# A streaming softmax: two loads merged into one, and three transfers released by a part of a group

## The chip, the cores and the metric

The kernel runs on one core of a Trainium2 chip. The metric is the device time of one execution in microseconds (us), the median of several runs. Beside it stands one profiled execution, whose trace gives the span of the program and what each engine and each DMA transfer did in it.

The engines named here are DVE (VectorE), ACT (ScalarE), POOL (GpSimd) and SP (SyncE, which here only waits and issues DMA). PE (TensorE) does nothing in this kernel.

## The reference

A softmax over the last axis of a float32 tensor of 16 x 1024 x 512:

```python
x_max = np.max(x, axis=-1, keepdims=True)
exp_x = np.exp(x - x_max)
return (exp_x / np.sum(exp_x, axis=-1, keepdims=True)).astype(np.float32)
```

Input and output have 33.55 MB each, so 67.11 MB pass between DRAM and the core's memory.

## The kernel before, in words

The 16384 rows of 512 numbers are spread over 128 partitions, so that each partition has 128 rows. In the kernel "row r" means the r-th row of every partition (128 x 512 numbers, 256 KB). Rows are worked on in 16 groups of 8 (`GROUP`): group g is rows 8g to 8g+7. The buffer `held` has room for 12 groups (`RING`, 96 rows), so rows 96 to 127 use the places of rows 0 to 31 again.

Rows are loaded and stored in larger transfers, all on one queue, SP's. `ORDER` lists them: "L" for a load, "S" for a store, with their rows. In this text a transfer is called by its first row: load 0, 16, 32, 48 (16 rows, 4 MB each), load 64 (32 rows, 8 MB), load 96 and 112 (4 MB); store 0, 16, 32, 48 (4 MB), store 64 and 96 (8 MB). The first five (`AHEAD`) are issued at the start, and the rest in the order of the list by SP, each after waiting for what it needs. `BLOCKS` says how rows lie in DRAM: the rows of a block are divided among the partitions so that each partition has one contiguous run, and a transfer of half a block takes half of each run (loads 96 and 112 do, from block 96 to 127).

What each issue waits for, on SP:

- a store waits for the groups in it to be scaled (semaphores `scaled[g]`),
- a load into places that are used again waits for the stores of what was there (`stored`),
- `AFTER` adds a wait: store 0 also waits for group 4, load 96 for group 8, load 112 for group 9, store 48 for group 11. These groups are not in the transfer; the wait only holds the issue back.

SP works through its list in order, so that a wait holds back everything behind it.

Each group goes through four steps, and the names below are used throughout:

- M (L167, DVE): `reduce_max` over the 8 rows, negated, after the load has landed.
- the exponential (L211, ACT): 8 activations, one for each row, in a loop over groups; each also sums its row. ACT takes one group after another and waits for M of the next.
- P's reciprocal (L175, DVE): one over the sums, after ACT's last row of the group.
- P's product (L181, POOL): the 8 rows times the reciprocals, one `tensor_mul` of 128 x 4096. Groups 14 and 15 do it on DVE instead (V14, V15).

The list `VECTOR` gives DVE's order of M, P and V steps. DVE carries it out strictly in this order, so that an M whose load hasn't landed holds back the reciprocals behind it.

Of the kernel before, what the change touches and what calls it, by code (L numbers as in the profile page):

```python
# [13 lines left out]
GROUP = 8  # L14
# [3 lines left out]

BLOCKS = [(0, 16), (16, 32), (32, 48), (48, 64), (64, 96), (96, 128)]
ORDER = [
    ("L", (0, 16)),
    ("L", (16, 32)),
    ("L", (32, 48)),
    ("L", (48, 64)),
    ("L", (64, 96)),
    ("S", (0, 16)),
    ("S", (16, 32)),
# [4 lines left out]
    ("S", (64, 96)),  # L34
    ("S", (96, 128)),
]
AHEAD = 5

AFTER = {("S", 0): 4, ("L", 96): 8, ("L", 112): 9, ("S", 48): 11}

VECTOR = """
    M0 M1 P0 M2 P1 M3 P2 M4 P3 M5 P4 M6 P5 M7 P6 M8 P7 M9 P8 M10 P9 M11
    P10 P11 M12 M13 P12 M14 P13 M15 V14 V15
"""

# [23 lines left out]
@with_exitstack  # L73
def kernel(
    ctx: ExitStack,
    tc: tile.TileContext,
    x: bass.AP,
    out: bass.AP,
):
    nc = tc.nc  # L80
    nc.at_finalize(loads_at_the_head)
    P = nc.NUM_PARTITIONS

    d = x.shape[-1]
    x_rows, out_rows = x.flatten_outer_dims(), out.flatten_outer_dims()
    assert x_rows.shape[0] == GROUPS * GROUP * P

    def in_dram(rows, a, b):

        first, last = next(k for k in BLOCKS if k[0] <= a and b <= k[1])  # L90
        block = rows[first * P : last * P].rearrange("(p r) d -> p r d", p=P)
        return block[:, a - first : b - first, :]

    held = nc.alloc_sbuf_tensor("held", [P, RING, d], F32).ap()
    shift = nc.alloc_sbuf_tensor("shift", [P, GROUPS * GROUP], F32).ap()
    sums = nc.alloc_sbuf_tensor("sums", [P, GROUPS * GROUP], F32).ap()
    recip = nc.alloc_sbuf_tensor("recip", [P, GROUPS * GROUP], F32).ap()

    loads = [k for what, k in ORDER if what == "L"]
    stores = [k for what, k in ORDER if what == "S"]  # L100
    loaded = {k: nc.alloc_semaphore(f"loaded{k[0]}") for k in loads}
    scaled = [nc.alloc_semaphore(f"scaled{g}") for g in range(GROUPS)]
    stored = {k: nc.alloc_semaphore(f"stored{k[0]}") for k in stores}
    maxed = nc.alloc_semaphore("maxed")
    expd = nc.alloc_semaphore("expd")
    to_pool = nc.alloc_semaphore("to_pool")
    to_vector = nc.alloc_semaphore("to_vector")

    def take(engine, semaphore, n):

        engine.wait_ge(semaphore, n).then_inc(semaphore, -n)  # L111

    def rows(a, b):
        assert a // RING == (b - 1) // RING
        return held[:, a % RING : (b - 1) % RING + 1, :]

    def meets(k, a, b):
        return k[0] < b and a < k[1]

    def group(g):  # L120
        return g * GROUP, (g + 1) * GROUP

    def stats(t, g):
        return t[:, g * GROUP : (g + 1) * GROUP]

    def load(k):
        copy = nc.sync.dma_start(out=rows(*k), in_=in_dram(x_rows, *k))
        copy.then_inc(loaded[k], 16)
        return copy

    with tc.manual_schedule():
        for _, k in ORDER[:AHEAD]:
            tc.no_tile_sem_insts.add(load(k).ins.name)
    tc.close()
    tc.compile()  # L138

    taken, done = set(), set()  # L140
    for what, k in ORDER[AHEAD:]:
        for g in range(GROUPS):
            due = AFTER.get((what, k[0])) == g or (what == "S" and meets(k, *group(g)))
            if due and g not in done:
                take(nc.sync, scaled[g], 1)
                done.add(g)
        if what == "L":
            for s in stores:
                if meets(s, k[0] - RING, k[1] - RING) and s not in taken:
                    take(nc.sync, stored[s], 16)  # L150
                    taken.add(s)
            load(k)
        else:
            nc.sync.dma_start(out=in_dram(out_rows, *k), in_=rows(*k)).then_inc(
                stored[k], 16
            )

    seen, given = set(), {}  # L160

    def rowmax(g):
        for k in loads:
            if meets(k, *group(g)) and k not in seen:
                take(nc.vector, loaded[k], 16)
                seen.add(k)
        nc.vector.reduce_max(  # L167
            out=stats(shift, g), in_=rows(*group(g)), axis=AX, negate=True
        ).then_inc(maxed, 1)

    def scale(g, engine, ready):

        if g == 0:
            take(nc.vector, expd, 1)
        ratio = nc.vector.reciprocal(out=stats(recip, g), in_=stats(sums, g))  # L175
        if g:
            ratio.wait_op(expd, g, "sem-ge")
        ratio.then_inc(ready, 1)
        if g == 0:
            take(engine, ready, 1)  # L180
        product = engine.tensor_mul(  # L181
            out=rows(*group(g)),
            in0=rows(*group(g)),
            in1=stats(recip, g).unsqueeze(2).to_broadcast([P, GROUP, d]),
        )
        if g:
            given[ready] = given.get(ready, 0) + 1
            product.wait_op(ready, given[ready], "sem-ge")
        product.then_inc(scaled[g], 1)

    for step in VECTOR.split():
        what, g = step[0], int(step[1:])
        if what == "M":
            rowmax(g)
        elif what == "V":
            scale(g, nc.vector, to_vector)
        else:
            scale(g, nc.gpsimd, to_pool)
    take(nc.vector, expd, GROUPS - 1)
    take(nc.vector, to_vector, given[to_vector])  # L200
    take(nc.gpsimd, to_pool, given[to_pool])


    nc.scalar.preload_act_table(EXP)  # L204

    with nc.scalar.Fori(0, GROUPS) as i:  # L206
        take(nc.scalar, maxed, 1)
        for r in range(GROUP):
            row = held[:, bass.ds(i % (RING // GROUP) * GROUP + r, 1), :]
            at = bass.ds(i * GROUP + r, 1)  # L210
            act = nc.scalar.activation(  # L211
                out=row,
                in_=row,
                func=EXP,
                bias=shift[:, at],
                scale=1.0,
                accum_out=sums[:, at],
            )
        act.then_inc(expd, 1)


    for k in stores:
        if k not in taken:
            take(nc.sync, stored[k], 16)
# [30 lines left out]
```

## Time and profile before

| | us |
|---|---|
| median of 3 runs (lowest to highest) | 159.46 (159.26 to 159.68) |
| profiled execution, its own time | 159.32 |
| its span in the trace | 158.0 |
| DVE, ACT, POOL busy | 83.8, 91.9, 97.9 |
| one product of a group on POOL (L181), mean of 14 | 7.016 |
| one reduction of a group on DVE (L167), mean of 16 | 4.396 |
| one exponential row on ACT (L211), mean of 128 | 0.713 |
| DMA queue q1, share of 16 engines' span | 99.0% |

The span runs from the first instruction to the last; the profiled execution's own time is 1.32 us more. The busy time of an engine counts its compute instructions alone; waiting and issuing DMA is not counted. The DMA share is how much of the time the packets of the 16 DMA engines took. Times in rows of a timeline are counted from the start of the span. A transfer is complete when it has landed, which its semaphore shows.

### The profile page before, as it was taken

To read this page: it belongs to the slowest core of one execution; us is meant where nothing else is said; L and a number is where in the kernel's file an instruction comes from. 1 tells how busy PE (TensorE), PEld (TensorE's weight loads), DVE (VectorE), ACT (ScalarE), POOL (GpSimd) and SP (SyncE) were. 2 spreads that over 40 slices of the span, in tenths; PEclk is the share of its full clock that TensorE was granted. 3 is DMA by queue.
4 is the path that set the end of the run, shared out by engine and by line. 5 is a ranking of instruction groups with operands and counts; after the bars stand their busy time and mean duration, and the time that the engine had idled before them with its cause. 6 is when DMAs were issued, how large, how long until landed. Compare 5 with 4: busy or idle time off the path is not lost. (4 is left out here: it accounts for less than half of the span.)

```text
span 158.0 us, 714 instructions
## 1 busy us (share of the span) xinstructions
DVE 83.8 (53%) x34; ACT 91.9 (58%) x257; POOL 97.9 (62%) x18
## 2 busy tenths in 40 slices
DVE  0008959778977916969760000695976998000000
ACT  1100699999999997499999300049999920000000
POOL 0000009999999999999999999991999600000000
DMA  7999999999969969999999999999999969969976
GB/s 265 465 465 398 398 473 456 398 398 489 572 265 531 498 299 398 456 465 407 398 465 465 373 423 398 431 481 415 398 514 415 531 265 531 498 299 531 465 332 265
DMA packets 1872, 67.11 MB, mean 425 GB/s; under 512 B 208, under 2 KB 208, under 8 KB 208
## 3 DMA queue, kind: packets, MB, share of 16 engines
q1 hardware_dynamic: 1872, 67.11, 99.0%
HBM read 33.55 MB, written 33.55 MB: 425 GB/s over the span
## 5 line engine op out<-in xcount | busy, mean ns | idle before, releaser
L181 POOL TENSOR_TENSOR held<-held,recip 128x4096 f32<-128x4096 f32 x14 | 97.7, 7016 | 26.8 <-POOLq L111 23.0
L211 ACT ACTIVATE held<-held,shift x128 | 90.3, 713 | 32.2 <-ACTq L111 32.2
L167 DVE TENSOR_REDUCE shift<-held 128x8 f32<-128x4096 f32 x16 | 70.2, 4396 | 27.8 <-DVEq L111 27.8
L211 ACT ACTIVATION_READ_ACCUMULATOR held<-held,shift x128 | 24.7, 193 | 0.0
L175 DVE RECIPROCAL recip<-sums 128x8 f32<-128x8 f32 x16 | 3.2, 202 | 22.1 <-ACT held L211 20.2
L181 DVE TENSOR_TENSOR held<-held,recip 128x4096 f32<-128x4096 f32 x2 | 11.4, 5725 | 0.1
L204 ACT ACT_TABLE_LOAD x1 | 1.3, 1283 | 3.5 <-PEq L138 3.5
L239 POOL MEMSET const-float32-0.0<- 128x1 f32 x1 | 0.1, 98 | 0.2 <-issue 0.2
L239 POOL MEMSET const-bfloat16-1.0<- 128x1 bf16 x1 | 0.1, 101 | 0.0
L239 POOL MEMSET const-uint8-127<- 128x1 uint8 x1 | 0.1, 101 | 0.0
L239 POOL MEMSET const-float32-1.0<- 128x1 f32 x1 | 0.1, 98 | 0.0
## 6 DMA issues: line engine op xcount, KB each, us to landing
held<-in_x_dram SPq DMA_DIRECT2D x6, 4096.0 KB, 18.7
out_dram<-held SPq DMA_DIRECT2D x4, 4096.0 KB, 16.5
out_dram<-held SPq DMA_DIRECT2D x2, 27.5
held<-in_x_dram SPq DMA_DIRECT2D x1, 58.4
```

The costliest lines, as they stand in the source:

```text
L167: nc.vector.reduce_max(out=stats(shift, g), in_=rows(*group(g)), axis=AX, negate=True).then_inc(maxed, 1)
L175: ratio = nc.vector.reciprocal(out=stats(recip, g), in_=stats(sums, g))
L181: product = engine.tensor_mul(out=rows(*group(g)), in0=rows(*group(g)), in1=stats(recip, g).unsqueeze(2).to_broadcast([P, GROUP, d]),)
L204: nc.scalar.preload_act_table(EXP)
L211: act = nc.scalar.activation(out=row, in_=row, func=EXP, bias=shift[:, at], scale=1.0, accum_out=sums[:, at],)
L239: nc = _bacc.Bacc("TRN2", target_bir_lowering=False, num_devices=1)
```

## The change

1. Rows 32 to 63 become one block and one load of 8 MB ("load 32" from here on; load 48 is gone). Four transfers are issued ahead, not five. Stores 32 and 48 are still two, and each now takes half of every partition's run in DRAM.
2. In DVE's order, P3 comes ahead of M4.
3. Three products on POOL (groups 4, 8 and 11) are split into two instructions: the first 7, 7 and 6 rows, and the rest. The first of each pair raises a new semaphore `begun`; store 0, load 96 and store 48 wait for it, in place of the whole group. Load 112 still waits for all of group 9. Store 32 still waits for all of groups 4 and 5, and store 64 for all of groups 8 to 11, because these are in them.

On POOL, 14 products become 17 instructions: 11 of 128x4096, two of 128x3584 with 128x512 behind each, and one of 128x3072 with 128x1024 behind it. On SP there is one load less, and the order of the others is the same.

```diff
-BLOCKS = [(0, 16), (16, 32), (32, 48), (48, 64), (64, 96), (96, 128)]
+BLOCKS = [(0, 16), (16, 32), (32, 64), (64, 96), (96, 128)]
 ORDER = [
     ("L", (0, 16)),
     ("L", (16, 32)),
-    ("L", (32, 48)),
-    ("L", (48, 64)),
+    ("L", (32, 64)),
     ("L", (64, 96)),
...
-AHEAD = 5
+AHEAD = 4
...
-AFTER = {("S", 0): 4, ("L", 96): 8, ("L", 112): 9, ("S", 48): 11}
+AFTER = {("L", 112): 9}
+AFTER_FIRST = {("S", 0): 4, ("L", 96): 8, ("S", 48): 11}
+FIRST = {4: 7, 8: 7, 11: 6}
...
 VECTOR = """
-    M0 M1 P0 M2 P1 M3 P2 M4 P3 M5 P4 M6 P5 M7 P6 M8 P7 M9 P8 M10 P9 M11
+    M0 M1 P0 M2 P1 M3 P2 P3 M4 M5 P4 M6 P5 M7 P6 M8 P7 M9 P8 M10 P9 M11
     P10 P11 M12 M13 P12 M14 P13 M15 V14 V15
 """
...
+        if (what, k[0]) in AFTER_FIRST:
+            take(nc.sync, begun, 1)
...
-        product = engine.tensor_mul(
-            out=rows(*group(g)),
-            in0=rows(*group(g)),
-            in1=stats(recip, g).unsqueeze(2).to_broadcast([P, GROUP, d]),
-        )
+        def multiply(a, b):
+            return engine.tensor_mul(
+                out=rows(a, b),
+                in0=rows(a, b),
+                in1=recip[:, a:b].unsqueeze(2).to_broadcast([P, b - a, d]),
+            )
+
+        first, last = group(g)
+        lead = FIRST.get(g, GROUP)
+        product = multiply(first, first + lead)
         if g:
             given[ready] = given.get(ready, 0) + 1
             product.wait_op(ready, given[ready], "sem-ge")
+        if lead < GROUP:
+            product.then_inc(begun, 1)
+            product = multiply(first + lead, last)
         product.then_inc(scaled[g], 1)
```

More of the change, by code (lines that the diff above doesn't have):

```diff
@@ L105 @@
     expd = nc.alloc_semaphore("expd")
+    begun = nc.alloc_semaphore("begun")
     to_pool = nc.alloc_semaphore("to_pool")
```

## The prediction

> **What bounds the kernel now.** I read the page first: engines, then the DMA queue.
>
> ```profile
> DVE 83.8 (53%) x34; ACT 91.9 (58%) x257; POOL 97.9 (62%) x18
> ...
> DMA  7999999999969969999999999999999969969976
> ...
> q1 hardware_dynamic: 1872, 67.11, 99.0%
> ```
>
> No engine is busy for two thirds of the span, and the one DMA queue is for 99.0% of it. The chain of waits on the page names V14 and V15 (L181 on DVE), yet it accounts for 19% of the span: it ends at 133.75, when the last store is issued, and the transfers after that are not in it. So I read the transfers one by one, from the answers on DMA issues in short windows (issue time from the timeline, plus the last column: us to landing). Stores 0, 16 and 32, then load 96:
>
> ```profile
> out_dram<-held SPq DMA_DIRECT2D x1, 4096.0 KB, 11.9
> ...
> out_dram<-held SPq DMA_DIRECT2D x1, 4096.0 KB, 21.0
> ...
> out_dram<-held SPq DMA_DIRECT2D x1, 4096.0 KB, 24.8
> ...
> held<-in_x_dram SPq DMA_DIRECT2D x1, 4096.0 KB, 13.5
> ```
>
> Issued at 58.47, 59.00, 65.44 and 86.43, they land at 70.4, 80.0, 90.2 and 99.9. The loads before them land at 12.2, 21.9, 31.6, 41.3 and 60.6, the transfers after them at 109.6, 119.4, 138.6 and 158.0, the end of the span. The distances are 9.7 for every transfer of 4 MB and 19.3 to 19.4 for every one of 8 MB, with one exception: store 32 needs 10.2. The queue is never empty after its first packet at 1.0 us; it loses 0.5 us once, where it turns from stores (32) to loads (96). In the packet records that loss is packets of 1.25 to 1.9 us instead of 1.213, starting between 87.6 and 90.8; nothing similar stands at the turns from loads to stores (60 and 109 us).
>
> So the time is: start, plus the sum of transfers, plus any time in which the queue has nothing. An engine matters only where an issue comes too late. The issues and the work that sets them, from the timeline in three windows:
>
> ```profile
> 51.35 13.99 POOL L181 TENSOR_TENSOR held<-held,recip 128x4096 f32<-128x4096 f32 x2
> 58.47 0.87 SPq L154 DMA_DIRECT2D out_dram<-held  x2
> 60.79 4.42 DVE L167 TENSOR_REDUCE shift<-held 128x8 f32<-128x4096 f32 x1 [3.82 <-DVEq L111]
> ...
> 86.43 0.34 SPq L127 DMA_DIRECT2D held<-in_x_dram  x1
> ...
> 107.28 0.82 SPq L154 DMA_DIRECT2D out_dram<-held  x2
> ```
>
> The first POOL row is P4 and P5: P4 ends at 58.37 and store 0 goes out 0.10 later. At the head, the first packet starts 1.02 us after the issue, on the slowest engine 1.94 (the packet records). Store 0's packets begin at 59.76 to 60.20, right behind load 64's. So 58.47 + 1.02 = 59.49 is 0.27 us ahead of need on the first engine, and by the head's slowest start there may be no margin at all. This is the tightest issue; load 96 and store 48 begin their packets 2.4 and 1.3 us or more after their issues.
>
> **The change, part by part.**
>
> *One transfer less.* Loads 32 and 48 (2 x 9.7 = 19.4) become one of 8 MB (19.3 to 19.4). The gain is 0 to 0.1 us. The packet records give it closer: 8 packets of 1.213 per DMA engine and transfer before, 8 of 2.418 after, so 16 x 1.213 - 8 x 2.418 = 0.06. It lies on the DMA queue, which sets the end, so it counts in full. The DMA page of the Trainium skill, "DMA: Bandwidth & Descriptors" (section "Anatomy of one DMA"), gives each DMA a fixed cost of about 2.0 us beside its bytes; by that the sum would be 2.0 us lower (see the rivals). It describes GpSimd's path, and this case's queue shows 4 MB every 9.7 us, without such a cost.
>
> *M4 waits for the whole block.* M4 started early before; now it needs landing 41.3 - 0.06 = 41.24. On DVE, M5 and P4's reciprocal are queued behind that wait, and on ACT group 4 waits for it. P3's reciprocal would be too, but the new order puts it ahead: it runs at 39.8 as before, and POOL takes P3 at 44.4. Now the steps, each from a row with the same wait:
>
> ```profile
> 65.55 0.72 ACT L211 ACTIVATE held<-held,shift  x1 [3.19 <-ACTq L111]
> ...
> 71.34 0.20 DVE L175 RECIPROCAL recip<-sums 128x8 f32<-128x8 f32 x1 [1.73 <-ACT held L211]
> ...
> 110.63 0.20 DVE L175 RECIPROCAL recip<-sums 128x8 f32<-128x8 f32 x1 [1.80 <-ACT held L211]
> ...
> 110.92 13.99 POOL L181 TENSOR_TENSOR held<-held,recip 128x4096 f32<-128x4096 f32 x2 [3.73 <-DVE recip L175]
> ```
>
> Landing to reduction: 60.6 to 60.79, 0.14 by the finer landing record, so M4 at 41.38. Reduction to the group's first exponential: 60.79 to 65.55, 4.76, so 46.14. To the reciprocal: 65.55 to 71.34, 5.79, so 51.93. To the product: 110.63 to 110.92, 0.29, so P4 starts at 52.22, 0.87 later than at 51.35. POOL was free at 51.35, so every later product up to P11 moves by 0.87. P12 waits for its reciprocal at 110.63 and POOL is free at 108.1, so the delay ends there.
>
> *Store 0 after 7 rows of P4.* 7/8 of 7.02 is 6.14; 52.22 + 6.14 + 0.10 = 58.46, against 58.47 before. The two parts cancel, and the queue reaches this point 0.06 earlier: cost 0, if the cover (up to 0.27) is not less than 0.05. Behind this wait on SP stand stores 16 and 32 and everything later. Without cover, each 0.1 us here is 0.1 us of the end.
>
> *Splits on POOL.* Each split adds one instruction. The small ones on POOL (the memsets) take 0.10 and start 0.03 to 0.04 apart; DVE's reciprocal of 8 elements takes 0.20. So 0.03 to 0.20 for one; I take 0.10, from POOL's own rows.
>
> *Load 96 after 7 rows of P8.* P8 would start at 79.25 + 0.87 + 0.10 = 80.22; 6.14 on is 86.36, issued at 86.50 against 86.43. Its first packets are due at 88.86. Cost 0.
>
> *Store 48 after 6 rows of P11.* 100.17 + 0.87 + 0.20 + 5.26 + 0.06 = 106.56, against 107.28: 0.7 earlier. It is due at 108.5 and cannot start sooner, since it queues behind load 112. Cost 0; a transfer that waits longer in the queue is seen at store 32 (issued 14 us ahead) without loss at its start.
>
> *Later issues.* Store 32 needs P5: 66.4 instead of 65.44, due at 79.1. Load 112 needs all of P9: 94.5 instead of 93.41, due at 98.9. Store 64 needs all of P11: 108.4, due at 118.3. Store 96 is set by V15 as before (133.86, due at 137.7). All keep 3 us or more.
>
> *Stores 32 and 48 in DRAM.* Their runs of 32 KB now stand 64 KB apart, because rows 32 to 63 are one block. Loads 96 and 112 have that layout and take 9.7 each; no store with it is shown. I take 0, with store 32's own excess of 0.5 each as the other end.
>
> The sum: -0.06, and the loss of 0.5 at the turn stays. The profiled execution took 159.32 (span 158.0 and 1.32 around it), 0.14 under the median of 159.46. So 159.26 for it, and 159.40 against the median. About 0.3% (0.48 us) is what a measurement of this kernel can tell from no change, so this is no change.
>
> **Rivals.**
>
> *The turn at 88 us costs something else.* Store 32's addresses and load 96's arrival change a little, and the stretched packets may be a matter of how both meet. Without the 0.5: 158.9. For: it is the only loss in the stream. Against: stores still turn to loads at the same moment. Chance 0.14.
>
> *Store 0 comes late (the slower side).* If the 7 rows take nearly as long as 8, store 0 goes out at 52.22 + 7.02 + 0.10 = 59.34; packets start at 60.36 at the earliest, where load 64 now ends at 59.70: 0.66 us of empty queue, 160.0. It decides from an issue at about 58.7 on, where the margin is used up; past 0.3% from 59.2. Against: POOL's products take 7.01 to 7.02 each and leave little room for a fixed part. Chance 0.09.
>
> *The spread stores run slower.* At 0.5 each: 160.4. The same page of the skill (section "Latency and other measured facts") reports lower rates for DRAM pitches of 512 KiB and more; 64 KB is not among them. Chance 0.06.
>
> *Store 48, queued 0.7 earlier, disturbs the end of load 112* as load 96 does at 88: 159.9. Against: no such stretch where store 0 follows load 64. Chance 0.05.
>
> *A fixed cost per transfer is saved.* As much as 2.0 us by the rule above, which would be 157.4; by the rows at most 0.1, which changes nothing. Chance of more than 0.3%: 0.02.
>
> **The numbers.** The forecast, 159.1 to 159.7, has 0.64. Faster by over 0.3%: 0.14 + 0.02 = 0.16. Slower: 0.09 + 0.06 + 0.05 = 0.20. The range of 158.8 to 160.1 holds the forecast, the turn without its loss, the late store 0 and the early store 48; it leaves out 160.4 and 157.4, 0.08 together.
>
> **What would show it.** Right: the merged load lands near 41.2; P4 starts near 52.2; store 0 is issued near 58.46 and lands 9.7 after load 64; store 48 near 106.6; POOL with rows of 128x3584 near 6.15; again one interval of 10.2 at store 32. Wrong: an interval over 9.8 at store 0, 48 or 32's start, a split product that costs over 0.3 more than a whole one, or store 32 without its excess.

## The result, and the profile after

The changed kernel takes 159.97 us (median of 21 runs, 159.59 to 161.00) against 159.44 for the kernel before (21 runs): a ratio of 1.0041, 95% interval 1.0030 to 1.0051. That is 0.53 us slower, above the bound of 0.3%. The forecast was 159.40, no change. The profiled execution took 159.88, its span is 158.6.

From the page of the changed kernel, the lines that answer to those of before (engine, busy us; then the DMA queue):

```profile
DVE 83.9 (53%) x34; ACT 92.1 (58%) x257; POOL 98.4 (62%) x21
...
DMA  7999998989969969999999999999999989989985
...
q1 hardware_dynamic: 1728, 67.11, 98.8%
```

The kernel is as bound by the DMA queue as before: 98.8% of a span that is 0.6 us longer. What was forecast for the engines came out. Timeline of the changed kernel, start and length in us; the POOL row joins P4's two parts and P5:

```profile
52.15 14.14 POOL L187 TENSOR_TENSOR held<-held,recip 128x3584 f32<-128x3584 f32 x3 [0.79 <-DVE recip L180]
...
58.41 0.87 SPq L159 DMA_DIRECT2D out_dram<-held  x2
...
86.52 8.31 SPq L130 DMA_DIRECT2D held<-in_x_dram  x2
...
106.67 2.19 SPq L159 DMA_DIRECT2D out_dram<-held  x2
```

P4 starts at 52.15 (forecast 52.2), store 0 goes out at 58.41 (58.46), load 96 at 86.52 (86.50), store 48 at 106.67 (106.56). So the time is in the transfers. DMA issues in short windows of the changed kernel, for store 0, store 16, store 32, load 96, load 112 and store 48 (last column: us from issue to landing):

```profile
out_dram<-held SPq DMA_DIRECT2D x1, 4096.0 KB, 11.8
...
out_dram<-held SPq DMA_DIRECT2D x1, 4096.0 KB, 21.0
...
out_dram<-held SPq DMA_DIRECT2D x1, 4096.0 KB, 23.9
...
held<-in_x_dram SPq DMA_DIRECT2D x1, 4096.0 KB, 13.6
...
held<-in_x_dram SPq DMA_DIRECT2D x1, 4096.0 KB, 15.7
...
out_dram<-held SPq DMA_DIRECT2D x1, 4096.0 KB, 13.2
```

With the issues at 58.41, 58.95, 66.39, 86.52, 94.50 and 106.67 these landings are 70.2, 80.0, 90.3, 100.1, 110.2 and 119.9. The same lines of the kernel before, for load 112 (issued at 93.41) and store 48 (107.28):

```profile
held<-in_x_dram SPq DMA_DIRECT2D x1, 4096.0 KB, 16.2
...
out_dram<-held SPq DMA_DIRECT2D x1, 4096.0 KB, 12.1
```

From the landing records, which are finer:

| landing of | before | interval | after | interval |
|---|---|---|---|---|
| store 16 | 80.03 | | 79.97 | |
| store 32 | 90.25 | 10.22 | 90.30 | 10.34 |
| load 96 | 99.95 | 9.71 | 100.13 | 9.83 |
| load 112 | 109.65 | 9.69 | 110.21 | 10.08 |
| store 48 | 119.35 | 9.70 | 119.92 | 9.71 |
| store 96, the end | 157.96 | | 158.52 | |

At store 16 the changed kernel is 0.06 ahead. Then it loses 0.12 + 0.12 = 0.24 more at the turn from stores to loads (88 us), and 0.39 at the turn from loads to stores (109 us), where the kernel before lost nothing. -0.06 + 0.24 + 0.39 = 0.57, against 0.56 at the end.

These are two single executions. The loss at the turn of 88 us differs a good deal from one to the next: store 32 and load 96 together take 19.93 in the kernel before, and 19.87 and 19.55 in two of its variants below whose load 96 has the same lead (the layout alone, and store 48 earlier alone). So the 0.24 by itself shows little, and for this turn the medians of the experiments have to decide.

The packet records show what the 0.39 is. Store 48 is issued at 106.67. Of load 112's last packets, one for each DMA engine, those that start from 107.75 on, 1.08 us later, take 1.24 to 1.81 us in place of 1.213 ("stretched" from here on); those that started earlier take 1.213. In the kernel before, store 48 was issued at 107.28 and none is stretched. Each of the 16 DMA engines has 8 packets of a 4 MB transfer, and the transfer has landed when the last engine is done.

### The profile page after: what moved, and what is told of

It reads as the page before. It is cut to its first block, busy times and chain, and to the rows that moved or that the text cites. A ratio compares the mean times of both kernels' runs of the same rounds, so it can differ in the third digit from the quotient of the medians.

```text
span 158.6 us, 718 instructions
## 1 busy us (share of the span) xinstructions
DVE 83.9 (53%) x34; ACT 92.1 (58%) x257; POOL 98.4 (62%) x21
## 3 DMA queue, kind: packets, MB, share of 16 engines
q1 hardware_dynamic: 1728, 67.11, 98.8%
## 5 line engine op out<-in xcount | busy, mean ns | idle before, releaser
L187 POOL TENSOR_TENSOR held<-held,recip 128x4096 f32<-128x4096 f32 (+4 forms) x17 | 98.2, 5813 | 26.5 <-POOLq L114 23.0
```

The lines of the kernel that those rows point to most:

```text
L187: return engine.tensor_mul(out=rows(a, b), in0=rows(a, b), in1=recip[:, a:b].unsqueeze(2).to_broadcast([P, b - a, d]),)
```

## The experiments

Each kernel ran beside the kernel before, whose median was 159.32 to 159.42 in these comparisons. The diffs show the settings that differ; where a variant of the kernel before splits a product, it also has the code for that. "Lead" below is how far ahead of the end of store 32 load 96 is issued: the profiled landing of store 16, plus 9.7, less the issue. It is 80.03 + 9.7 - 86.43 = 3.30 in the kernel before and 3.15 in the changed one. The expectations, written before the runs, count leads from the first packet and so give smaller numbers.

**Store 48 after 7 rows of group 11.**

```diff
-FIRST = {4: 7, 8: 7, 11: 6}
+FIRST = {4: 7, 8: 7, 11: 7}
```

> The changed kernel with one edit: store 48 follows the first 7 rows of group 11 in place of 6, so it is issued near 107.55 in place of 106.67, and its first packet can start near 108.57, where load 112 ends at 108.7 to 109.2. Theory A (a transfer of the other direction that reaches the queue while the last packets of the one before are still to start stretches these packets): none of load 112's last packets is stretched, load 112 and store 48 land 9.7 apart from their neighbours, and the time falls by 0.3 to 0.5 us, to 159.5 to 159.7. Rival B (the 64 KB pitch of stores 32 and 48 in DRAM costs the time): no change, 160.0. Rival C (the merged load or the later load 112 costs it): no change, 160.0.

Measured: 159.69, ratio 1.0019 (1.0009 to 1.0028), whose interval lies below that of the changed kernel. Load 112's line, issued at 94.90:

```profile
held<-in_x_dram SPq DMA_DIRECT2D x1, 4096.0 KB, 15.2
```

It lands at 110.14, 9.70 after load 96, and none of its last packets is stretched: theory A for this turn. Measured against the kernel before, the loss falls from 0.53 to 0.28 us, so 0.25 of it is the row by which store 48 is earlier. The rest stays.

**The kernel before, with store 48 earlier alone.**

```diff
-AFTER = {("S", 0): 4, ("L", 96): 8, ("L", 112): 9, ("S", 48): 11}
+AFTER = {("S", 0): 4, ("L", 96): 8, ("L", 112): 9}
+AFTER_FIRST = {("S", 48): 11}
+FIRST = {11: 7}
```

> The kernel before with one edit: product 11 on POOL is split after 7 rows and store 48 follows these, so it is issued near 106.4 in place of 107.28, 2.1 us ahead of the first packet that it can start. Blocks, loads and DVE's order are those of before. Theory A (early arrival of the other direction): load 112's last packets, those that start after 107.4, are stretched, and the time rises by 0.3 to 0.5 us to 159.75 to 159.95. Rivals B (pitch in DRAM) and C (merged load): as before, 159.45.

Measured: 159.59, ratio 1.0009 (0.9998 to 1.0021): 0.18 us more, less than expected, and the interval just reaches no change, so the time alone doesn't show a loss. In its profile twelve of load 112's last packets are stretched, from 107.43 on (issue 106.70), and the interval of load 112 is 9.91 in place of 9.69. The stretch is there without any other part of the change.

**Store 48 much earlier: after group 10.**

```diff
-AFTER = {("L", 112): 9}
-AFTER_FIRST = {("S", 0): 4, ("L", 96): 8, ("S", 48): 11}
-FIRST = {4: 7, 8: 7, 11: 6}
+AFTER = {("L", 112): 9, ("S", 48): 10}
+AFTER_FIRST = {("S", 0): 4, ("L", 96): 8}
+FIRST = {4: 7, 8: 7}
```

> The changed kernel with store 48 after the whole of group 10, issued near 101.3, 5.3 us earlier than after 6 rows of group 11 and some 7 us ahead of its first packet. Theory A (each packet of load 112 that starts after the arrival is stretched): four or five packets per DMA engine are stretched in place of one, 160.5 to 161.5. A weaker form of A (only the last packet is stretched, however early the arrival): 159.95, as the changed kernel. Rival (early arrival costs nothing, and the gain from 7 rows came from elsewhere): 159.7.

Measured: 160.97, ratio 1.0103 (1.0089 to 1.0118). Load 112, issued at 94.71, and store 48, issued at 101.61:

```profile
held<-in_x_dram SPq DMA_DIRECT2D x1, 4096.0 KB, 16.6
out_dram<-held SPq DMA_DIRECT2D x1, 4096.0 KB, 19.4
```

Load 112 now takes 10.82. But theory A's form was wrong: packets that start between 102.6 (the arrival) and 106.2 are not stretched. The stretched ones start from 106.2 to 109.1; they are the last one or two of load 112 on each DMA engine. So an early store 48 makes the turn itself dearer, 1.1 us here against 0.4 with 6 rows and 0 with 7. It doesn't slow the load while it waits.

**Layout alone.** One block in DRAM, and still two loads of 4 MB:

```diff
-BLOCKS = [(0, 16), (16, 32), (32, 48), (48, 64), (64, 96), (96, 128)]
+BLOCKS = [(0, 16), (16, 32), (32, 64), (64, 96), (96, 128)]
```

> The kernel before with one edit: rows 32 to 63 are one block in DRAM, but still two loads of 4 MB, and every issue is where it was. Theory A (early arrival of the other direction): as before, 159.45, since nothing moves in time. Rival B (pitch of loads and stores 32 and 48): store 32 or store 48 takes over 9.8 and the time is 159.9 to 160.4. Rival C (merged load): as before, 159.45.

Measured: 159.51, ratio 1.0008 (0.9997 to 1.0018). If the pitch of stores 32 and 48 costs anything, it is not over 0.3 us, and no cost is shown.

**Load 96 after the whole of group 8.**

```diff
-AFTER = {("L", 112): 9}
-AFTER_FIRST = {("S", 0): 4, ("L", 96): 8, ("S", 48): 11}
-FIRST = {4: 7, 8: 7, 11: 6}
+AFTER = {("L", 96): 8, ("L", 112): 9}
+AFTER_FIRST = {("S", 0): 4, ("S", 48): 11}
+FIRST = {4: 7, 11: 6}
```

> The changed kernel with one edit: load 96 follows the whole of group 8 again, so it is issued near 87.4 in place of 86.52 and can start near 88.4, after the last packets of store 32 have started (87.5 to 88.0) and before they end (88.8 to 89.3). Theory A (early arrival of the other direction): the last packets of store 32 are no longer stretched; the time falls by 0.2 to 0.5 us, to 159.5 to 159.8, with the stretch at load 112's end still there. Rival D (the turn from stores to loads costs 0.5 by itself, whenever the load is queued): no change or a little more, 160.0 to 160.2. Rivals B and C: 160.0.

Measured: 161.57, ratio 1.0127 (1.0098 to 1.0156). All theories were wrong here: a load that comes 0.97 us later, but still in time, costs 1.6 us. Load 96 takes 11.07 and load 112 11.04. One thing that theory A expected did happen: store 32's last packets are hardly stretched (its interval is 9.69). But load 96's first packets are, to as much as 2.51 us, so the loss moved from the store to the load and grew. As an account of the time, theory A does not hold for the turn from stores to loads.

**Load 96 earlier in the merged kernel.** Two runs, both with store 48 after 7 rows: load 96 after 5 rows of group 8 (the diff), and after the whole of group 7 (product 8 whole again).

```diff
-FIRST = {4: 7, 8: 7, 11: 7}
+FIRST = {4: 7, 8: 5, 11: 7}
```

> The changed kernel with store 48 after 7 rows of group 11 (159.69 before this edit) and load 96 after 5 rows of group 8 in place of 7: load 96 is issued near 85.0, 1.75 us earlier, 4 us ahead of its first packet. Theory E (load 96 comes too late for some DMA engines: one sits idle for 0.3 to 0.65 us near 89 us in the changed kernel and in the run with store 48 moved, and none does before): no idle engine at 89 us, 159.3 to 159.45. Theory A (an early arrival of the other direction stretches packets) for this turn: one more packet per DMA engine of store 32 is stretched, 160.0 or more. Rival D (the turn from stores to loads costs 0.5 to 0.8 whenever the load is queued): 159.7.

> As the run before this one, but load 96 follows the whole of group 7, so it is issued near 80.4, 8.5 us ahead of its first packet, with all eight packets per DMA engine of store 32 still to run. Theory E (late for some DMA engines): as with 5 rows, 159.3 to 159.45. Theory A (early arrival stretches every packet that starts after it): all of store 32's packets are stretched, 160.5 to 162. Rival D (the turn costs the same whenever): 159.7.

Measured: 160.89, ratio 1.0095 (1.0077 to 1.0113), and 160.98, ratio 1.0105 (1.0091 to 1.0120). Theory E falls. With the load queued from 80.5, up to five DMA engines at a time still stand idle between 89.3 and 90.1. This idle time is part of the turn and no sign of a late issue. Rival D falls too, since the turn's loss depends on the issue: load 96's interval is 11.0 and 11.3 in these runs, 9.89 with 7 rows.

**Store 0 after the whole of group 4.**

```diff
-AFTER_FIRST = {("S", 0): 4, ("L", 96): 8, ("S", 48): 11}
-FIRST = {4: 7, 8: 7, 11: 7}
+AFTER_FIRST = {("L", 96): 8, ("S", 48): 11}
+FIRST = {8: 7, 11: 7}
```

(with `("S", 0): 4` back in `AFTER`)

> The changed kernel with store 48 after 7 rows of group 11 (159.69 before this edit) and store 0 after the whole of group 4: it is issued near 59.3 in place of 58.45. By the prediction's price the queue is empty for 0.66 us behind load 64, store 0 lands 10.3 to 10.4 after load 64, and the time is 160.3 to 160.4. Rival (the first 7 rows give nothing, since the queue had a margin): 159.7.

Measured: 160.34, ratio 1.0061 (1.0048 to 1.0074), 0.65 us over the run without this edit. Timeline and store 0's DMA line:

```profile
59.36 0.87 SPq L159 DMA_DIRECT2D out_dram<-held  x2
```

```profile
out_dram<-held SPq DMA_DIRECT2D x1, 4096.0 KB, 11.2
```

The total is as expected, its place is not. Store 0 lands at 70.54, 9.92 after load 64, only 0.21 more than without this edit (9.71) and not at 10.3 to 10.4. On the first DMA engines the queue is empty from 59.6 to 60.2, and all sixteen start within 0.15 us of each other; the rest of the loss appears later, at store 32 (10.56 against 10.24), store 48 and store 64. Packets start 0.85 to 1.00 us after the issue here, and not up to 1.94 as at the head, which answers for store 0 the cover that the prediction left open. It is no fixed figure: in the run with store 48 after 7 rows some DMA engines are done with load 112 and idle from 108.81 on, and the last of them starts on store 48 at 109.28, 1.34 us after its issue.

**How much the time of load 96 matters.** In the kernel before, load 96 was moved by small amounts: later by splitting products 6 and 7 (0.15 us each), earlier by letting it follow the first columns of group 8 in place of rows.

```diff
+FIRST = {6: 7, 7: 7}
```

> The kernel before (two loads of 4 MB, separate blocks, whole groups ahead of store 0 and store 48) with POOL's products 6 and 7 split into 7 rows and 1: each split costs 0.13 us, so load 96 goes out near 86.7 in place of 86.43, and its lead over its first packet falls from 2.4 to 2.15 us, as in the run with store 48 after 7 rows. Theory F (the turn from stores to loads at 88 us loses the least for a lead near 2.4 us, and tenths of a us of lead count): 159.6 to 159.8, with the loss in store 32's and load 96's intervals. Rival B (layout of block 32 to 63) and rival C (merged load): as before, 159.4.

The same, with store 48 kept at its time by a split of product 11 by columns, 492 of 512 and then 20:

```diff
-AFTER = {("S", 0): 4, ("L", 96): 8, ("L", 112): 9, ("S", 48): 11}
+AFTER = {("S", 0): 4, ("L", 96): 8, ("L", 112): 9}
+AFTER_FIRST = {("S", 48): 11}
+FIRST = {6: 7, 7: 7}
+COLUMNS = {11: 492}
```

> The kernel before with products 6 and 7 split so that load 96 is issued near 86.7 in place of 86.43 (as the run that gave 160.15), and product 11 split by columns (492 of 512) so that store 48 is still issued near 107.3, as before. Theory F (load 96's lead alone makes the loss): 160.0 to 160.3, as with both later. Rival (store 48, which also went out 0.3 us later in that run, made the loss): 159.4.

Earlier, after 484 and after 456 of the 512 columns of group 8 (`COLUMNS` cuts a group's product in two: all 8 rows by the first columns, then by the rest):

```diff
-AFTER = {("S", 0): 4, ("L", 96): 8, ("L", 112): 9, ("S", 48): 11}
+AFTER = {("S", 0): 4, ("L", 112): 9, ("S", 48): 11}
+AFTER_FIRST = {("L", 96): 8}
+COLUMNS = {8: 484}
```

> The kernel before with POOL's product 8 split by columns (484 of 512, then 28) and load 96 after the first part: issued near 86.05 in place of 86.43, a lead of 2.8 us. Theory F: the loss moves by a few tenths; toward the 160.9 of the runs with leads of 4 and 8 us if the best lead is near 2.4, so 159.6 to 160.0; below 159.4 if the best lead lies above 2.4. Rivals B and C: as before, 159.4.

> The kernel before with load 96 after 456 of 512 columns of group 8: issued near 85.75, a lead of 3.15 us, where 484 columns (2.85 us) gave 159.27. Theory F with its best lead between 2.4 and 2.9: 159.5 to 159.9, on the way to 160.9 at 4 us. Rival (any lead over 2.4 us is as good): 159.3.

Measured: 160.15, ratio 1.0049 (1.0030 to 1.0067), both later; 160.01, ratio 1.0040 (1.0026 to 1.0055), load 96 alone later. So load 96 is the cause of this loss, which is larger than the 0.2 to 0.4 that theory F gave for it. With both later the single executions lie from 159.32 to 161.14, far wider than the kernel before (159.14 to 159.83). Earlier: 159.27 with 484 columns, ratio 1.0001 (0.9985 to 1.0016), one of its 11 runs at 160.52; and 159.72 with 456, ratio 1.0032 (1.0018 to 1.0047). Theory F holds in the kernel before: by lead, 0.3 us later costs 0.7, 0.4 earlier is no worse, 0.8 earlier costs 0.4.

The same edit by 484 columns together with the `BLOCKS` of the layout run:

> The kernel before with load 96 after 484 of 512 columns of group 8 (159.27) and rows 32 to 63 as one block in DRAM, loaded by two transfers. Rival B (the pitch of stores 32 and 48 is what remains of the loss in the changed kernel after both issues are moved, 0.17 us): 159.4 to 159.5. Rival C (it comes with the merged load and the work that it makes late): 159.27.

Measured: 159.36, ratio 1.0008 (0.9994 to 1.0022). Again no cost of the layout beyond 0.1 us that could be told from nothing.

**The same in the merged kernel,** with store 48 after 7 rows: load 96 after 428 and after 402 columns of group 8.

```diff
-FIRST = {4: 7, 8: 7, 11: 7}
+FIRST = {4: 7, 11: 7}
+COLUMNS = {8: 428}
```

> The changed kernel with store 48 after 7 rows of group 11 (159.69 before this edit) and product 8 split by columns (428 of 512) in place of 7 rows of 8: load 96 goes out 0.27 us earlier, with a lead of 2.45 us as in the kernel before. Theory F (the lead of load 96 sets what is left of the loss): 159.3 to 159.45. Rivals B (layout) and C (merged load): 159.7.

> The changed kernel with store 48 after 7 rows of group 11 and load 96 after 402 of 512 columns of group 8, issued near 86.1, a lead of 2.85 us, which is the lead of the best run so far (159.27). Theory F (the leads alone make the difference): 159.2 to 159.3, 0.06 under that run for the transfer less. Rivals B and C: 159.5 to 159.6, as with 428 columns.

Measured: 159.59, ratio 1.0023 (1.0004 to 1.0042), and 161.05, ratio 1.0102 (1.0088 to 1.0117). The first misses theory F by little, but its interval covers that of 7 rows (1.0009 to 1.0028), so a gain from the better lead is not shown in the merged kernel. The second contradicts theory F, for the lead of 3.65 us is what served best without the merged load (3.68).

**The merged load taken apart again, everything behind it left late.**

```diff
-    ("L", (32, 64)),
+    ("L", (32, 48)),
+    ("L", (48, 64)),
...
+            due = meets(k, *group(g)) or (g == 4 and k[0] == 48)
```

> The run that gave 161.05 (merged load, load 96 after 402 columns of group 8, store 48 after 7 rows), with the merged load taken apart again into two of 4 MB; M4 still waits for both, so that every later step of DVE, ACT and POOL stands where it stood. Rival C, first form (the 8 MB transfer itself upsets the turn at 88 us): 159.3 to 159.5. Rival C, second form (the later compute does, for instance ACT working until 91.3 us, through the turn, in place of 88.1): 160.7 to 161.2.

> The changed kernel with store 48 after 7 rows of group 11 (159.69), with the merged load taken apart again into two of 4 MB and M4 still waiting for both. First form of rival C (the 8 MB transfer): 159.4. Second form (the later compute): 159.75, 0.06 more than with the merged load.

Measured: 159.47 with 402 columns, ratio 1.0011 (0.9999 to 1.0022), and 159.76 with 7 rows, ratio 1.0025 (1.0015 to 1.0034). Load 96's lines with 402 columns, merged (issue 86.01) and taken apart (86.20):

```profile
held<-in_x_dram SPq DMA_DIRECT2D x1, 4096.0 KB, 15.3
```

```profile
held<-in_x_dram SPq DMA_DIRECT2D x1, 4096.0 KB, 13.9
```

Load 96 takes 11.23 in the first and 9.93 in the second, although it is issued with nearly the same lead (3.65 and 3.71) and ACT works through the turn in both, to 91.3 and 91.5. So the later compute is not the cause at this lead. What is left that differs is the one transfer of 8 MB at 21 to 41 us, 45 us ahead of the turn, and 0.06 us of lead. The two ran on different chips; but on the chip of the merged run, two loads with the same layout and a lead of 3.67 (the layout run with 484 columns) stood at +0.04, so the chip alone is not it. How a load could act on a turn 45 us later is not shown. With 7 rows, near the changed kernel, it makes no such difference: 159.69 merged, 159.76 with two loads, the 0.06 that was forecast for a transfer less, though the intervals overlap.

These two runs with two loads also test theory F once more. They ran side by side, all later work is late in both, and they differ in product 8's split alone: +0.39 at a lead of 3.07, +0.10 at 3.71. Here the lead is worth about 0.3 us, though the intervals overlap a little, and late work with a good lead cannot be told from no change.

**An early load 96 without the merged load.**

```diff
-AFTER = {("S", 0): 4, ("L", 96): 8, ("L", 112): 9, ("S", 48): 11}
+AFTER = {("S", 0): 4, ("L", 96): 7, ("L", 112): 9, ("S", 48): 11}
```

> The kernel before with one edit: load 96 follows group 7 in place of group 8, so it is issued near 79.45 in place of 86.43, 9.4 us ahead of its first packet. The merged kernel with this early load gave 160.98. If the early arrival by itself makes the turn at 88 us dear (theory F): 160.6 to 161.1. If only the merged kernel is so sensitive, as with 402 columns (161.05 merged, 159.47 with two loads): 159.3 to 159.8.

Measured: 159.80, ratio 1.0039 (1.0021 to 1.0056), at the upper end of the second expectation. Being early costs 0.43 here, and 1.6 with the merged load.

The runs above that compare times of load 96, by lead; the time is the median's distance to that of the kernel before in the same comparison:

| lead, us | two loads | merged load |
|---|---|---|
| 2.23 | | +2.16 (store 48 early as well) |
| 3.00 to 3.01 | +0.73, +0.69 | |
| 3.07 to 3.15 | +0.39 | +0.28, +0.53 (the changed kernel, store 48 early) |
| 3.30 to 3.35 | 0, +0.10 (layout) | +0.17 |
| 3.65 to 3.71 | -0.15, +0.04, +0.10 | +1.73 |
| 4.07 | +0.40 | |
| 4.85 | | +1.54 |
| 9.2 to 10.3 | +0.43 | +1.63 |

## Why the prediction was wrong

*What bounds the kernel, and the way to count:* right. Every part of the 0.56 us of the profile is an interval between landings; no engine became the bound.

*One transfer less, 0.06:* right in the profile. The merged load lands 19.35 after load 16; the two loads took 9.71 + 9.71 = 19.42. (That store 16 lands 0.06 earlier is not the same 0.06: 0.05 of it is there when load 0 lands, and store 16 takes 9.72 in place of 9.66.)

*M4 and its chain:* right within 0.1 us at each step. *Store 0:* right: 58.41 against 58.46, no gap. The price of being late (0.66) was measured as 0.65, in part by luck: 0.21 of it stands at store 0, where the prediction put all of it, and the rest behind it.

*Splits on POOL:* 7.02 became 6.166 + 1.041, and P8 starts 0.15 later for one split; 0.10 was taken, within the bounds.

```profile
L187 POOL TENSOR_TENSOR held<-held,recip 128x3584 f32<-128x3584 f32 x2 | 12.3, 6166 | 0.8 <-DVE recip L180 0.8
...
L187 POOL TENSOR_TENSOR held<-held,recip 128x512 f32<-128x512 f32 x2 | 2.1, 1041 | 0.0
```

(The two numbers behind the first bar are the busy time in us and the mean of one in ns.)

*"Store 48 ... Cost 0":* the first step that failed. It was 0.39 in the profile, 0.25 in the medians. The prediction took store 32, issued 14 us ahead without loss, as the row for a transfer that waits in the queue. But that is a store behind a store. For a store behind a load the nearest rows were store 0 and store 48 themselves, both issued hardly more than 1 us ahead of their first packets, and they said nothing of a longer wait. The rival that named this place had 0.5 us and a chance of 0.05: the right mechanism, too little weight. That its 159.9 is near the measured 159.97 is luck, since only about half of the loss is store 48's.

*"Load 96 ... Cost 0":* the second. Issued as forecast, its lead fell by 0.15 us (0.09 from the later issue, 0.06 from the shorter queue), and the turn lost 0.24 more in the profile. The prediction had seen this turn as the only loss in the stream, and yet let it stay constant or vanish. That it could grow was not weighed, and with two loads it grows on both sides of a window of some 0.4 us. The remaining 0.28 of the medians, with store 48 put right, is of the size that two loads show for such a lead (+0.39 at 3.07, against +0.10 at 3.71 with all else the same). The layout shows no cost, and with 7 rows the merged load none. In the merged kernel itself the lead is not shown to be the cause: moved back to 3.35 it left +0.17, which cannot be told from +0.28, and moved on to 3.65 it made +1.73.

*The other rivals:* store 0 late did not happen. Slower spread stores are not shown. The fixed cost per transfer of 2.0 us, which the Trainium skill's page "DMA: Bandwidth & Descriptors" (section "Anatomy of one DMA") gives for one DMA on GpSimd's path, does not appear in this full queue: the profile shows 0.07 saved (19.42 against 19.35).

*The range* held the result (158.8 to 160.1), by the rivals on the slow side; the sign was missed.

What stays open: why the turn depends on tenths of a us of lead, and why the merged load makes it so much dearer at some leads and not at others. The profile shows which packets are stretched and which DMA engines wait. It does not show the cause, and no run here separates one.

## What to carry to other kernels

When one DMA queue is full from end to end, count intervals between landings, and look for the transfers where it turns from stores to loads or back. In this kernel the moment at which the first transfer of the other direction enters the queue has a price there: for a load behind stores on either side of a narrow best value, for a store behind loads when it comes early or too late. A wait that only holds an issue back, tuned for one set of times, has to be tuned again when anything ahead of it moves by a few tenths of a us. An issue that comes earlier is not free merely because it queues, and the row that would show its cost must have the same direction change.

## What the runs showed of the hardware

- A store that follows loads was free when issued 1.05 to 1.3 us ahead of its first packet (the kernel before, and store 48 after 7 rows), cost 0.2 to 0.4 us at 2.0 to 2.2 us (store 48 earlier alone, and the changed kernel), and 1.1 us at 8 us: the last packets of the load are stretched from 1.213 to as much as 2.1 us. This holds where the turn ahead was left as it was. Behind a dearer turn at 88 us (load 96 alone later; after 5 rows; after 402 columns with the merged load) load 112 took 10.2 to 10.3, although store 48 was issued only 1.1 to 1.6 us ahead.
- A load that follows stores lost something in every profile here: store 32 and load 96 together took 0.2 to 2.1 us over 19.4, and DMA engines stand idle in the turn even when the load was queued 9 us before.
- With the queue empty, packets of a store started 0.85 to 1.00 us after its issue at store 0, and up to 1.34 us after it at store 48.
- POOL's product takes 1.041, 1.894, 5.311, 6.166 and 7.018 us for 512, 1024, 3072, 3584 and 4096 elements of a partition: 0.19 fixed and 0.85 for each row of 512. A split costs 0.15, a little less than the fixed part, because the next instruction starts 0.04 before the one ahead has ended (P5 at 58.33 in the kernel before, where P4 ends at 58.37).
